# Letting the state space and convolution steps precede the projections in the planner's order

## The chip, the cores and the metric

The kernel runs on one core of a Trainium2 chip. The metric is device microseconds of one execution. Three runs of the kernel before took 1490.85, 1486.84 and 1486.92 us, a median of 1486.92. Engines are called as in the profile: PE is TensorE's matmul side (PEld its weight loads), DVE is VectorE, ACT is ScalarE, POOL is GpSimd and SP is the engine whose queue issues nearly all DMAs.

## The reference, cut to what matters

Two layers run over 256 latent and 256 context tokens of width 1024. The change lies in the mixer of layer 0:

```python
p_lat = h_lat @ w_in                      # 1024 -> 3*768 + 256; the same for the context tokens
u = p[..., -256:]                         # to the state space branch (S5)
st_f, st_b = s5_scan(u, ...)              # 16 groups, 64 complex states, both directions
y_s5 = s5_readout(u, st_f, st_b, ...)     # gelu, then a gated linear unit
uc = short_conv(p[..., :3 * 768], ...)    # three taps, then x1, x2, v of 768 channels each
z = x1 * fft_conv(v, kf[:, 0], bias[0])   # a long convolution by transform, product, inverse
y_hy = x2 * fft_conv(z, kf[:, 1], bias[1])
x = x + m[2] * (concat([y_hy, y_s5]) @ w_out)
```

A mixture of experts, layer 1 (a gated recurrence and its own experts) and a norm follow; the change does not touch their code.

## The kernel before, in words

Everything is kept transposed, channels on the 128 partitions and the 512 tokens along the free dimension. Weights of the projections are split into two parts (`whi` on ACT, `wlo` on POOL or DVE), and each product is three matmuls of 128x512.

`layer0_mixer` (L1304) runs two streams of work. The **fill** (`pipeline`, L1265) is a list of independent jobs: `Channels` (L1162) computes 128 channels of the in projection with the short convolution, `Mods` (L1203) multiplies a block of the modulation weights, `Out` (L1225) computes 128 columns of the out projection from some of the 8 channel blocks. Each job splits its weights (`prep`), runs its matmuls (`mms`) into one of two PSUM banks `in_t`, and finishes on ACT, DVE and POOL (`after`). The **main** stream is a chain. First comes the state space branch `s5_mixer` (L889), four quarters of four groups each: tables `Gt` on DVE and `Hm` on POOL (`s5_quarter_tables`, L822), the product `U`,`Gm` and the scan on DVE that ends in `prev` (`s5_state`, L971), the matrix `Km` (matmuls `Hm`,`wB`, copied to `KX` and moved by 8 DMAs of SP, L874), and the readout `U`,`Km` and `prev`,`Hm`; then `s5_glu` (L931). Then `convs` (L1438) takes six units of 128 channels in the order 4, 5, 0, 1, 2, 3. A unit is two convolutions (`hyena_conv`, L1090): matmuls `zv`,`dft`, a stretch of DVE work (`Z`, `t`, `Z`, `yy`) with two products `t` on POOL, and the inverse matmuls `yy`,`dft`. In between it computes the filter of the unit after it (`hyena_spectra`, L1036: tiles `hw`, `sd`, `nv`, `K`).

`drive` (L209) writes the two streams into one program: it takes a step of the main stream, which ends in a `yield` of some microseconds, then takes jobs of the fill until their own estimates make up that gap. The gaps are 5.0 (L911), 4.5 (L913), 3.8 (L927) and less in a quarter, 6.5 (L1118) after the products of a convolution, 0.9 and 0.8 in between. The gaps of the state space part add up to 63.4, the fill jobs listed first (10 `Channels` of 5.12 and 8 `Mods` of 1.83) to 65.8. The gaps of the convolutions add up to 100.2, the fill left for them (without the last eight `Out` jobs, which need unit 3) to about 101.

The order on each engine is not the order of the program alone. A planner gives each instruction a number as it is written and plays the program through a model of the machine; whenever an engine is free there, it takes the ready instruction with the lowest number. The order that results is fixed: on the chip each engine works through its queue, and an instruction whose input is late holds those behind it. `E.first()` (L126) rewinds the counter to zero for the instructions written inside it, and restores it after. The kernel before uses it in the start of layer 0, in the routing and in layer 1, not in `drive`.

Of the kernel before, what the change touches and what calls it, by code (L numbers as in the profile page):

```python
# [2 lines left out]

# [1 line left out]

# [183 lines left out]
def run(g):  # L189
    for _ in g:  # L190
        pass


def steps(g, n):
    for _ in range(n):
        next(g, None)
# [9 lines left out]
        yield  # L206


def drive(main, fill):  # L209


    for gap in main:
        while gap > 0:
            c = next(fill, None)
            if c is None:
                break
            gap -= c
# [12 lines left out]
def mm3(E, o, w, h, ks, n0=0, n=T, first=True, last=True):  # L230

    for i, k in enumerate(ks):
        E.mm(o, w[0][:, k, :], h[0][:, k, n0:n0 + n], first and i == 0, False)
        E.mm(o, w[0][:, k, :], h[1][:, k, n0:n0 + n], False, False)
        E.mm(o, w[1][:, k, :], h[0][:, k, n0:n0 + n], False, last and i == len(ks) - 1)
# [653 lines left out]
def s5_mixer(E, o, hT, ycat, tabs, ws, hp, tp, wp):  # L889

    inp = []
    for m in range(2):
        b = E.bank("s5")
        mm3(E, b, ws[m], hT, range(KD))
        uT = wp.tile([P, T], F32, tag="uT", name="uT")
        E.act(uT, b, AF.Copy)
        yield 0.7
        if m == 0:
            Gm = next(tabs)
        inp.append((yield from s5_input(E, o, m, uT, wp, tp)))  # L900
    for m in range(2):
        U, ud = inp[m]
        y = wp.tile([P, 8, 64], F32, tag="uT", name="y5")
        for i in range(2):
            q = 2 * m + i
            if q:
                Gm = next(tabs)
                yield 1.2
            sl = slice(4 * i, 4 * i + 4)
            prev = s5_state(E, o, q, U[:, sl], Gm, wp)  # L910
            yield 5.0  # L911
            Hm, Km = next(tabs)
            yield 4.5  # L913
            b = E.bank("s5")
            for g in range(4):
                oo = b[:, g * 64:(g + 1) * 64]
                E.mm(oo, Km[:, g, :], U[:, 4 * i + g, :], True, False)
                E.mm(oo, Hm[:, 0, g, :], prev[:, 0, g, :], False, False)
                E.mm(oo, Hm[:, 1, g, :], prev[:, 1, g, :], False, True)
            E.tt(y[:, sl], b[:, :256].rearrange("p (g c) -> p g c", c=64), ud[:, sl], ADD)  # L920
            if i == 1:
                yield 0.7
                yield from s5_output(E, m, y, ycat, tp)
            if q < 3:
                tabs = s5_quarter_tables(E, o, q + 1, hp, tp)
                next(tabs)
                yield 3.8  # L927
    E.dump('ys5', ycat[:, 6:8])


def s5_glu(E, ycat, tp):  # L931
    gw = tp.tile([P, 2, 512], F32, tag="Gt", name="gw")
    E.SY.dma_start(gw, E.a['s5_glu_w'][0].rearrange("(k p) n -> p k n", p=P))
    yield 0
    glb = E.prm['glb']
    ag = []
    for m in (2, 3, 0, 1):
        b = E.bank("s5")
        for k in range(2):
            E.mm(b, gw[:, k, m * P:m * P + P], ycat[:, 6 + k, :], k == 0, k == 1)  # L940
        ag.append(b)
    for m in range(2):
        sg = tp.tile([P, 512], F32, tag=f"t{'xy'[m]}", name="sg")
        E.act(sg, ag[m], AF.Sigmoid, bias=glb[:, 2 + m:3 + m])
        E.stt(ycat[:, 6 + m, :], ag[2 + m], glb[:, m:m + 1], sg, ADD, MUL)


def s5_input(E, o, m, uT, wp, tp):

    UT = tp.tile([64, 8, 8, 16], F32, tag="Gt", name="UT")  # L950
    uv = uT.rearrange("p (c j) -> p j c", j=8)
    for h in range(2):
        b = E.bank("s5")
        for i in range(4):
            E.tr(b[:64, i * P:(i + 1) * P], uv[:, 4 * h + i, :])
        E.copy(UT[:, :, 4 * h:4 * h + 4, :].rearrange("p g j n -> p j g n"),
               b[:64].rearrange("p (j g n) -> p j g n", j=4, g=8))
    yield 1.5
    U = wp.tile([P, 8, 64], F32, name="U", bufs=2)
    b = E.bank("s5")  # L960
    for g in range(8):
        E.tr(b[:, g * 64:(g + 1) * 64], UT[:, g].rearrange("p j n -> p (j n)"))
    bv = b.rearrange("p (g c) -> p g c", c=64)
    E.act(U[:, :, 0:32], bv[:, :, 32:64], AF.Copy)
    E.act(U[:, :, 32:64], bv[:, :, 0:32], AF.Copy)
    ud = wp.tile([P, 8, 64], F32, name="ud", bufs=2)
    E.tt(ud, U, bcast(o.dcol[:, 8 * m:8 * m + 8], 2, 64), MUL, E.G)
    return U, ud
# [47 lines left out]
def s5_output(E, m, y, ycat, tp):  # L1016
    E.act(y, y, AF.Gelu_apprx_tanh)
    yield 0.8
    YT = tp.tile([64, 8, 8, 16], F32, tag="Gt", name="YT")
    for h in range(2):  # L1020
        b = E.bank("s5")
        for i in range(4):
            E.tr(b[:64, i * P:(i + 1) * P], y[:, 4 * h + i, :])
        E.copy(YT[:, :, 4 * h:4 * h + 4, :].rearrange("p j g n -> p g j n"),
               b[:64].rearrange("p (g j n) -> p g j n", g=4, j=8))
    yield 1.5
    b = E.bank("s5")
    for j in range(8):
        E.tr(b[:, j * 64:(j + 1) * 64], YT[:, j].rearrange("p g n -> p (g n)"))
    bv = b.rearrange("p (j s c) -> p s c j", j=8, s=2)  # L1030
    yv = ycat[:, 6 + m, :].rearrange("p (s c j) -> p s c j", s=2, j=8)
    E.act(yv[:, 1], bv[:, 0], AF.Copy)
    E.act(yv[:, 0], bv[:, 1], AF.Copy)
# [270 lines left out]
def layer0_mixer(E):  # L1304
    class O:
        pass
    o = O()
# [6 lines left out]
    with ExitStack() as l0:  # L1314
        E.psum(l0, "left", **{"in": (1, 2), "tr": (1, 1)})
        pl = l0.enter_context(E.pool("p_l0", 1))
        ycat = pl.tile([P, KD, T], F32, name="ycat")
# [4 lines left out]
        hT = [p_h.tile([P, KD, T], F32R, tag=f"h{i}", name=f"h0_{i}") for i in range(2)]  # L1322
# [3 lines left out]
        hp = E.hp = s5s.enter_context(E.pool("s5h", 1, "right"))  # L1326
        tq = E.tq = s5s.enter_context(E.pool("s5t", 1, "right"))
# [59 lines left out]
        with E.pool("boot", 1) as E.bp, E.pool("s5a", 1, "right") as E.tp:  # L1387
            tabs, ws = boot(E, o, feed, hT, hdn2)
# [7 lines left out]
        def more():  # L1396
            yield from first
            yield from jobs
            yh.extend(p_h.tile([P, KD, T], F32R, tag=f"h{i}", name=f"yh{i}") for i in range(2))
            for ks in ((4, 5, 6, 7), (0, 1), (2,), (3,)):  # L1400
                for i in range(8):
                    yield Out(E, feed, i, ks, yh, ycat, tmp, lambda ks=ks: done.issuperset(ks), tail if ks[0] == 3 else None)
                if ks[0] in (4, 0):
                    yield between.pop(0)
                    yield between.pop(0)
# [15 lines left out]

        fill = pipeline(more())
        wp = s5s.enter_context(E.pool("s5w", 1, "right"))
        drive(s5_mixer(E, o, hT, ycat, tabs, ws, hp, tq, wp), fill)
        drive(s5_glu(E, ycat, tq), fill)
        done.update((6, 7))
        s5s.close()
        hys = ExitStack()
        E.psum(hys, "right", hs=(2, 1), pd=(1, 3))
        with hys, E.pool("hyzb", 2, "right") as zb, E.pool("hyk", 2, "right") as kp, E.pool("hyt", 1, "right") as tp, \  # L1430
                E.pool("hyw", 2, "right") as wp:
            zp.update({u: zb for u in (0, 1)})
            E.dft = zb.tile([P, 8, P], F32, name="dft", bufs=1)
            E.SY.dma_start(E.dft, a['k_dft'])
            order = (4, 5, 0, 1, 2, 3)
            filt = {}

            def convs():  # L1438
                for _ in hyena_spectra(E, 4, hdn2, kp, tp, filt):
                    yield 3.0  # L1440
                for i, u in enumerate(order):
                    if i == 5:
                        tags = {"wge": ("fw3", 512), "bge": ("win", 256), "wA": ("hw", 1024), "lT": ("so", 512)}
                        ends["r"] = Route(E, 0, T // P, E.mT[0], lambda nm: tp.tile([P, tags[nm][1]], F32, tag=tags[nm][0], name=nm))
                        ends["r"].prepare(E.bank("hs")[:, 0])
                    spec = hyena_spectra(E, order[i + 1], hdn2, kp, tp, filt) if i < 5 else iter(())
                    steps(spec, 1)
                    while ("x1", u) not in zt:
                        next(fill)
                    yield from hyena_unit(E, u, *filt[u], zt["v", u], zt["x1", u], ycat, wp, spec)  # L1450
                    done.add(u)
                    run(spec)
                    yield 0.5

            drive(convs(), fill)
            run(fill)
    E.dump('ycat', ycat)
    E.dump('x1', E.xT)
# [677 lines left out]
def kernel(ctx: ExitStack, tc: tile.TileContext, a, out, dbg=None, stop=None):  # L2136
# [9 lines left out]
    with E.pool("ring", 3) as E.ring, E.pool("mod", 1) as E.mod:  # L2146
        layer0_mixer(E)
# [45 lines left out]
```

## Time and profile before

| | |
|---|---|
| median of 3 runs | 1486.92 us |
| the profiled execution, device time | 1486.51 us |
| its span | 1484.7 us |
| granted clock of PE, mean over the span | 0.932 |
| PE busy over the span | 87% |
| DVE, POOL, ACT busy over the span | 55%, 27%, 26% |

The span is the profiled part of an execution; 1.8 us of the device time lie around it. Busy shares are averages over stages with different limits. A row of the timeline gives the start in us from the span's start, the length, the engine, the line, the operation, the tile written and those read, the shape, how many were merged, and in brackets how long the engine had been idle before it and for whom. A granted clock of 1.00 is the full 2.4 GHz of PE, 0.50 the half.

### The profile page before, as it was taken

The page shows a single profiled execution, that of the slowest core. Times are in us where ns is not written, and L with a number is a line of the kernel's source. Part 1 is how long each engine was busy: PE and PEld are TensorE (multiplying, and loading weights), DVE is VectorE, ACT ScalarE, POOL GpSimd, SP SyncE. Part 2 cuts the span into 40 slices and gives each one's busy share as a digit, 9 for nine tenths or more (in the row PEclk, how much of TensorE's full clock was granted, in tenths as well). Part 3 has the DMA queues.
Part 4 walks back from the last instruction along what each step waited for, and adds up shares of the span by engine and source line. Part 5 has one row for each costly group of instructions (what it writes and reads, how often), then busy time and mean ns, then how long its engine had stood idle before and what let it go on. Part 6 is the DMA issues. An engine that isn't in the chain of part 4 may idle for free. (4 is left out here: it accounts for less than half of the span.)

```text
span 1484.7 us, 18755 instructions
## 1 busy us (share of the span) xinstructions
PE 1285.4 (87%) x7093; PEld 826.7 (56%) x7093; DVE 809.5 (55%) x1785; ACT 387.5 (26%) x655; POOL 400.0 (27%) x326
## 2 busy tenths in 40 slices
PE   6499999898886769999999498979798969999995
PEld 4266766575665443444444277878778733444443
DVE  5856554766666453344335685665656553343443
ACT  2233433132232321111111443333333312121211
POOL 2733431334554321111100452323231221111101
PEclk9699999899988779999999698999999979999998
DMA  8415673145121389999994111211213189999970
GB/s 298 181 57 183 225 259 142 57 144 218 42 91 79 117 340 416 393 388 384 383 385 175 43 62 53 78 64 59 84 60 122 65 339 395 418 419 420 419 314 31
DMA packets 55747, 311.91 MB, mean 210 GB/s; under 512 B 14441, under 2 KB 19994, under 8 KB 24282
## 3 DMA queue, kind: packets, MB, share of 16 engines
q1 hardware_dynamic: 50746, 303.72, 52.2%
q0 software_dynamic: 4608, 6.30, 1.3%
q8 instruction: 61, 1.00, 0.3%
q10 hardware_dynamic: 288, 0.52, 0.1%
q14 instruction: 44, 0.36, 0.1%
HBM read 315.76 MB, written 4.19 MB: 215 GB/s over the span
## 5 line engine op out<-in xcount | busy, mean ns | idle before, releaser
L148 PE MATMUL pg_t<-w,Xe 128*64 128x512 f32 x1024 | 228.7, 599 | 0.0
L148 PE MATMUL in_t<-h,whl 128*128 128x512 f32 (+1 forms) x768 | 147.2, 349 | 3.2 <-DVE h L158 2.4
L148 PEld LDWEIGHTS pg_t<-w,Xe 128*64 128x64 f32 x1024 | 71.1, 138 | 135.7 <-issue 131.1
L161 POOL TENSOR_TENSOR whl<-wraw,whl 128x2048 fp32r<-128x2048 f32 x20 | 93.6, 4684 | 175.6 <-ACT whl L155 175.6
L148 PEld LDWEIGHTS in_t<-h,whl 128*128 128x128 f32 x768 | 121.7, 195 | 22.1 <-POOL h L161 3.1
L148 PE MATMUL py_t<-w,hid 128*64 128x512 f32 x512 | 119.1, 606 | 4.2 <-DVE yl L161 3.0
L164 DVE SCALAR_TENSOR_TENSOR sg<-sg,ws,pg_t 128x256 f32<-128x256 f32 x32 | 15.4, 480 | 180.2 <-ACT sg L155 180.2
L1615 POOL MEMSET Xg<- 128x1024 f32 x32 | 30.4, 959 | 295.6 <-PE ga_t L152 295.6
L164 DVE SCALAR_TENSOR_TENSOR xT<-sc_t,mT,xT 128x256 f32<-128x256 f32 x204 | 90.3, 479 | 29.6 <-PE sc_t L148 28.1
L161 POOL TENSOR_TENSOR wlo<-w,whi 128x1024 fp32r<-128x1024 f32 (+3 forms) x51 | 72.0, 1416 | 107.6 <-ACT whi L155 100.7
L148 PE MATMUL sc_t<-OT,yh 128*128 128x512 f32 (+1 forms) x256 | 90.7, 369 | 10.2 <-DVE xT L164 7.6
L148 PE MATMUL in_t<-h,whi 128*128 128x512 f32 x288 | 97.6, 416 | 2.1 <-ACT ms L155 1.4
L148 PE MATMUL sc_t<-OT,yl 128*128 128x512 f32 (+1 forms) x256 | 82.6, 337 | 0.0
L148 PEld LDWEIGHTS sc_t<-OT,yh 128*128 128x128 f32 x256 | 48.0, 188 | 54.2 <-issue 27.9
L148 PEld LDWEIGHTS py_t<-w,hid 128*64 128x64 f32 x512 | 34.1, 138 | 64.8 <-issue 55.9
L155 ACT ACTIVATE yh<-py_t 128x1024 fp32r<-128x1024 f32 (+1 forms) x34 | 33.1, 974 | 121.5 <-PE py_t L148 117.3
L168 DVE TENSOR_SCALAR OT<-ht_t,ksq 128x512 fp32r<-128x512 f32 (+1 forms) x32 | 19.7, 616 | 81.5 <-PE ht_t L148 81.5
L155 ACT ACTIVATE sg<-pg_t 128x256 f32<-128x256 f32 x32 | 12.3, 385 | 195.3 <-PE pg_t L148 195.2
L148 PEld LDWEIGHTS in_t<-h,whi 128*128 128x128 f32 x288 | 51.5, 190 | 17.9 <-issue 5.2
L148 PE MATMUL at_t<-QA,X 128*128 128x128 f32 x224 | 37.5, 318 | 26.9 <-DVE QA L161 26.9
L1670 POOL DMA_INDIRECT Xg<-rows,ix x32 | 32.3, 1010 | 104.9 <-DVE ws L1676 33.4
L148 PE MATMUL in_t<-whl,h 128*128 128x256 f32 x384 | 56.5, 300 | 3.7 <-POOL whl L161 3.7
(442 smaller groups left out, 2446.1 us busy)
## 6 DMA issues: line engine op xcount, KB each, us to landing
w<-in_w_gu_dram SPq DMA_DIRECT2D x128, 1024.0 KB
w<-in_w_dn_dram SPq DMA_DIRECT2D x64, 1024.0 KB
w<-in_w_mod_dram SPq DMA_DIRECT2D x24, 2048.0 KB
wraw<-in_w_in_dram SPq DMA_DIRECT2D x20, 1024.0 KB
w<-in_w_in_dram SPq DMA_DIRECT2D x5, 2048.0 KB
w<-in_w_out_dram SPq DMA_DIRECT2D x2, 2048.0 KB
cwo<-in_w_out_dram SPq DMA_DIRECT2D x2, 2048.0 KB
rows<-hh SPq DMA_DIRECT2D x6, 512.0 KB
```

What stands on the lines that cost most here:

```text
L148: self.TE.matmul(o, l, r, start=st, stop=sp)
L155: self.S.activation(o, i, f, **k)
L161: (e or self.V).tensor_tensor(o, x, y, op=op)
L164: self.V.scalar_tensor_tensor(o, x, s, y, op0=op0, op1=op1)
L168: (e or self.V).tensor_scalar(o, x, s1, None, op0=op0)
L1615: E.G.memset(X, 0.0)
L1670: E.G.indirect_dma_start(X, None, rows, bass.IndirectOffsetOnAxis(ix[:, pi:pi + 1], 0), bounds_check=n - 1, oob_is_err=False)
```

## The change

`drive` takes an argument `E`. With it, each step of the main stream is written inside `E.first()`, so that its instructions get numbers from zero on; the fill keeps its numbers. The order in which the program is written, the gaps, the jobs, the tiles and the instructions stay. The three calls in layer 0 (state space, gated unit, convolutions) pass `E`; there is no other caller.

```diff
-def drive(main, fill):
-
-
-    for gap in main:
+def drive(main, fill, E=None):
+
+
+    while True:
+        with E.first() if E else nullcontext():
+            gap = next(main, None)
+        if gap is None:
+            return
         while gap > 0:
             c = next(fill, None)
             if c is None:
...
-        drive(s5_mixer(E, o, hT, ycat, tabs, ws, hp, tq, wp), fill)
-        drive(s5_glu(E, ycat, tq), fill)
+        drive(s5_mixer(E, o, hT, ycat, tabs, ws, hp, tq, wp), fill, E)
+        drive(s5_glu(E, ycat, tq), fill, E)
...
-            drive(convs(), fill)
+            drive(convs(), fill, E)
             run(fill)
```

## Rows read from the trace of the kernel before

**Rows 1.** The page's head and part 1: busy us, share of span, instructions.
```profile
span 1484.7 us, 18755 instructions
...
PE 1285.4 (87%) x7093; PEld 826.7 (56%) x7093; DVE 809.5 (55%) x1785; ACT 387.5 (26%) x655; POOL 400.0 (27%) x326
```
**Rows 2.** Windows: stretch, length, busy us per engine, granted clock, DMA share, GB/s.
```profile
80.00:240.00 160.00, 153.81 (x1007) 110.83 (x1006) 82.98 (x144) 56.03 (x96) 58.93 (x38) 1.00 0.51 186
240.00:475.00 235.00, 206.92 (x972) 146.16 (x972) 155.67 (x329) 62.23 (x119) 97.33 (x77) 0.92 0.30 110
475.00:512.00 37.00, 26.12 (x137) 13.87 (x137) 15.53 (x36) 9.23 (x21) 16.36 (x18) 0.82 0.13 38
```
**Rows 3.** Waits of PE, 240 to 475: us in total, times, longest.
```profile
PE pd_t L148 <- DVE yy L161: 15.0, 6, 4.0
PE hs_t L148 <- DVE hw L161: 11.3, 5, 3.3
```
**Rows 4.** Timeline of PE: one quarter of the state space branch.
```profile
169.25 1.90 PE L148 MATMUL s_t<-U,Gm 128*128 128x64 f32 x16
...
177.09 0.55 PE L148 MATMUL s_t<-Hm,wB 64*16 64x112 f32 x4
...
191.90 0.33 PE L148 MATMUL s_t<-U,Km 128*128 128x64 f32 x2
```
**Rows 5.** Timeline of SP's queue: the DMAs of that quarter.
```profile
180.81 7.64 SPq L874 DMA_DIRECT2D Km<-KX  x8
```
**Rows 6.** Timeline of PE: one inverse of a convolution.
```profile
364.70 1.13 PE L148 MATMUL pd_t<-yy,dft 128*128 128x256 f32 x4 [2.64 <-DVE yy L161]
365.48 1.10 PE L148 MATMUL in_t<-yh,whi 128*128 128x512 f32 x2
...
372.05 1.02 PE L148 MATMUL pd_t<-yy,dft 128*128 128x256 f32 x4
```
**Rows 7.** Timeline of PE: first, eleventh and twelfth wait, and what follows.
```profile
266.73 1.99 PE L148 MATMUL hs_t<-fw,hdn 64*128 64x256 f32 x4 [3.13 <-DVE hw L161]
...
465.11 2.93 PE L148 MATMUL pd_t<-yy,dft 128*128 128x256 f32 x6 [4.00 <-DVE yy L161]
...
473.39 1.46 PE L148 MATMUL pd_t<-zv,dft 128*128 128x256 f32 x6
481.31 3.78 PE L148 MATMUL pd_t<-yy,dft 128*128 128x256 f32 x8 [6.47 <-DVE yy L161]
485.78 0.74 PE L152 MATMUL tr_t<-ksq,yo 128*128 128x128 f32 x4 [0.69 <-ACT yo L155]
488.16 0.76 PE L148 MATMUL in_t<-yh,whi 128*128 128x512 f32 x2 [1.63 <-ACT yh L155]
489.51 0.79 PE L148 MATMUL in_t<-yh,whi 128*128 128x512 f32 x1 [0.59 <-POOL yh L161]
...
496.04 0.73 PE L148 MATMUL in_t<-yh,whi 128*128 128x512 f32 x2
```
**Rows 8.** Timeline of PE: the start of the state space branch.
```profile
83.99 0.50 PE L148 MATMUL in_t<-h,wlo 128*128 128x512 f32 x1 [1.32 <-POOL wlo L161]
...
88.97 0.73 PE L148 MATMUL s_t<-h,whi 128*128 128x512 f32 x2
```
**Rows 9.** Timeline of POOL: splits of weights and the start of a table.
```profile
66.02 2.38 POOL L161 TENSOR_TENSOR wlo<-w,whi 128x1024 fp32r<-128x1024 f32 x1
...
154.59 1.29 POOL L161 TENSOR_TENSOR Hm<-ux,uy 128x512 f32<-128x512 f32 x1 [0.52 <-PE s_t L148]
...
176.82 2.60 POOL L161 TENSOR_TENSOR wlo<-w,whi 128x1024 fp32r<-128x1024 f32 x1
```
**Rows 10.** Timeline of DVE: the end of the scan in two quarters.
```profile
177.25 3.90 DVE L161 TENSOR_TENSOR prev<-tA,tB 64x256 f32<-64x256 f32 x6
...
210.66 1.85 DVE L161 TENSOR_TENSOR prev<-tA,tB 64x256 f32<-64x256 f32 x6
```
**Rows 11.** Timeline of PE: the norm of the first filter.
```profile
252.43 1.95 PE L148 MATMUL hs_t<-ones,hw 128*128 128x1 f32 x16 [0.85 <-ACT hw L155]
```

More of the change, by code (lines that the diff above doesn't have):

```diff
@@ L1 @@
 import math
-from contextlib import ExitStack
+from contextlib import ExitStack, nullcontext
 import numpy as np
```

## The prediction, made before the changed kernel ran

> **What bounds the kernel now.** I read the page first: PE is busy 87% of the span [rows 1], so a reordering inside one stage can give back only what PE loses there. Then the windows of the stage that the change touches [rows 2]. From 80 to 240 us, beside the state space branch, PE is busy 153.8 of 160 us at the full clock: this stretch is bound by PE's work, and moving its steps changes the order of the work, not its amount. From 240 to 475 us, beside the convolutions, PE is busy 206.9 of 235 and its granted clock is 0.92: 28.1 us idle, and 16% of the time at the lower of the two levels. From 475 to 512 us it is busy 26.1 of 37 at 0.82. DMA is far from full in all three. So what can be won is at most the 6.2, 28.1 and 10.9 us idle and half of what runs at the lower clock.
>
> The waits say for whom PE idles [rows 3]: 15.0 us for `yy` in 6 waits and 11.3 us for `hw` in 5. The timeline shows that there is one such wait per convolution, twelve in all; the first eleven add up to 26.3 us, 2.4 each, the twelfth is 6.47 [rows 7]. Behind the waiting matmuls the fill follows, as at 365.48 [rows 6], with its inputs long ready: the planner put the main step at the head of PE's queue when its model had the input ready, and on the chip the input came later.
>
> **What the change moves.** No instruction is added or removed. It decides only where a main step and a fill step are both ready and the fill was written first. Where is that so in the trace?
>
> *State space.* In the third quarter the matmuls of `Km` start at 177.09, 5.9 us after `U`,`Gm` ended at 171.15 [rows 4], though they need only `Hm` and a free buffer; the gap of 5.0 stands between them in the program. In the four quarters the distance is 5.5, 7.3, 5.9 and 3.2 us (the row of one stands for the pattern). `Km` then takes 8 DMAs, 7.64 us of issue [rows 5], and its readout starts at 191.90. With the change these matmuls go right behind `U`,`Gm`, so each quarter shortens by about 4 to 8 us; with the second input block, whose matmuls at 88.97 can go some 5 us earlier [rows 8], I estimate the branch to end about 30 us sooner, near 210 instead of 240.
>
> *Convolutions.* At 364.70 four of the eight inverse matmuls run, then the fill until 372.05, then the other four [rows 6]: 6.3 us lost to the chain, the gap of 6.5. Four of the twelve inverses are split in this way by 6 to 7 us, and two start 4 to 5 us after `yy` (the row of one stands for the pattern). That is about 35 us of chain. Together the last convolution would end some 60 us earlier, near 425 instead of 485.
>
> That is time of the chain, not of PE, which runs the fill meanwhile. It is worth what PE loses at the end, where the fill is used up. After 473.39 nothing of the fill is left; PE waits 6.47 us for `yy`, 0.69, 1.63 and 0.59 us for the steps behind it, and runs at half clock until 496.04 [rows 7]. With 60 us of fill behind the chain this is what goes:
> - the twelfth wait becomes one like the others: 6.47 - 2.39 = 4.1 us;
> - 0.69 + 1.63 + 0.59 = 2.9 us;
> - 489.51 to 496.04 at full instead of half clock: 6.5 / 2 = 3.2 us.
>
> At the start, PE waits 1.32 us for the first `wlo` of the fill while the matmuls of 88.97 stand by [rows 8]; their weights were split by 68.4 [rows 9]. They can fill it: 1.3 us. The gains add up to 11.5 us.
>
> The eleven waits stay. They are the chip's lateness against the planner's model along the chain, and the chain has as many steps as before.
>
> **What it costs.** A main step that had the fill as cover now waits on PE at the instant at which the model has it ready, and all that is queued on PE waits with it.
>
> *Scan.* `Km` was last in the quarters; with it earlier, `prev` is. Its six operations take 1.85 us in one quarter and 3.90 in another [rows 10], where POOL was splitting weights at the same time [rows 9]. If the model has the short value, PE waits up to 2.1 us a quarter for this, and up to 4 if another DVE step is hit as well; it may also wait for nothing, as it does not wait at any readout now. I take 1.0 us, four times: 4 us, with bounds of 0 and 16.
>
> *Small steps of a unit.* `zv` to the second convolution, `yo` to its transposes, `hw` to the norm: three in each of six units, 18 in all, which mostly have cover now. The one that waits, waits 0.85 us [rows 11]; the others nothing. Bounds 0 and 15 us; I take 0.13 each, 2.4 us, near the many that do not wait.
>
> *Other queues.* On SP the DMAs of `Km` and the loads of the filters pass loads of fill weights, by up to 7.64 us [rows 5]; no wait of PE for a weight load shows in the three stretches, since three buffers run ahead, so nothing; without that cover it would be 7.6 us a quarter. On POOL the table operations from 154.59 on [rows 9] (five more behind it, 7 us) pass splits of the fill; they did so already, and PE's waits for `wlo` are 2.0 us in 80 to 240. Nothing, with 6 us as the upper bound. On DVE and ACT the main steps were mostly written ahead of the fill beside them. Nothing below zero is excluded: after the change more of the convolutions run beside `Channels`, and the first four waits, which lie there, average 2.0 us against 2.6 for the next seven. That could give 4 us; I leave it in the range.
>
> The sum: -11.5 + 4 + 2.4 = -5.1 us on the profiled execution, 1486.51 - 5.1 = 1481.4 us. That execution lies 0.4 us under the median of the runs, which I neglect: **1481 us**. What comes after the mixer starts earlier by the same amount and is otherwise the same.
>
> A rule of the Trainium skill speaks against this change: TensorE: Matmul & The Clock Gate (The mechanism) states that matmuls are in strict order in start and end, with no reordering. By it every main matmul placed too early holds all of the fill behind it, as the rows show at 465.11 [rows 7], and moving 30 more steps to their earliest place would only add waits: that is the third rival below.
>
> **The rivals.**
>
> *It gains more.* The waits shrink, since the chain now runs beside `Channels` with fewer operations on POOL per matmul, and fewer of them drop the clock. Against it: the first four convolutions already run there and wait 2.0 us on the mean, 3.13 in the first [rows 7]. If twelve waits of 1.2 us remain, 14 us go of the idle time and some 5 us of half clock besides, less than the full cost of the new waits: 1466 us.
>
> *It does almost nothing.* The planner already takes the main step first at most places, since the main stream runs behind the program; what moves is chain time which PE does not feel, and the end is bound by the last `Out` jobs, each with a split and an addition on POOL, instead of by the chain. For it speaks that eleven of twelve waits are already at the instant of readiness. 1486 us, give or take 4.
>
> *It is slower.* The mechanism is the one of the cost part: on PE's queue in order, steps that had the gaps as cover now each hold the fill. Four quarters with three steps each (`Gt`, `U`,`Gm`, readout) and 18 small ones make 30 places. At 0.85 us each [rows 11], 25 us, and the clock, which is at 1.00 from 80 to 240 now [rows 2], may fall after the longer ones. Against 11.5 us of gain it decides from 0.38 us per place on. At 0.7 us it gives 21 - 11.5 = +9.5: 1496 us. Against it: at the readouts, which interrupt a fill job in all four quarters and so were placed at the instant of readiness, PE does not wait now.
>
> **How the numbers follow.** A measurement of this kernel can tell about 0.3%, 4.5 us, from no change: faster is under 1482.5, slower over 1491.4. The forecast (1474 to 1487 by the nearer bounds of its costs) has a chance of 0.42, the larger gain 0.14, nothing 0.21, slower 0.23. The forecast falls on the faster side with 0.31 of its 0.42 and within with the rest, nothing falls within, with 0.02 on either side, and slower is over the bound with 0.21: faster 0.47, same 0.30, slower 0.23. The range goes from 1465, just under the larger gain, to 1497, just over the slower case.
>
> **What would show it.** In the profile after: the matmuls `Hm`,`wB` within 2 us of `U`,`Gm`; the last `s_t` readout before 200 us; no inverse split by fill; the last `pd_t<-yy` before 440 us, and a stretch of `Out` jobs behind it in which PE is busy throughout at clock 1.00; the last transpose of the mixer (510.4 us before) near 505. About twelve waits of PE on `yy` and `hw`, 25 to 30 us in all. It is wrong if PE's idle time from 80 to 240 grows beyond 12 us, if the chain's end does not move by 30 us or more, or if the chain ends early and PE still idles in the last 40 us.

## The result, and the profile after

| | before | after |
|---|---|---|
| median of 4 runs | 1487.47 us (1486.84 to 1490.85) | 1531.46 us (1529.14 to 1532.78) |
| ratio after to before | | 1.0289, 95% interval 1.0268 to 1.0311 |
| span of the profiled execution | 1484.7 us | 1527.4 us |

The change makes the kernel 44 us slower. The forecast was 1481, with a range up to 1497; sign and size were both wrong.

Of the page of the changed kernel, the line that answers to [rows 1]:

```profile
span 1527.4 us, 18764 instructions
...
PE 1313.1 (86%) x7093; PEld 833.9 (55%) x7093; DVE 814.8 (53%) x1785; ACT 387.1 (25%) x655; POOL 398.9 (26%) x326
```

The same 7093 matmuls now keep PE busy 27.7 us longer. That is the first hint: there are no more of them, so some took longer. The windows of the changed kernel, PE alone (stretch, length, busy us and matmuls, granted clock, DMA share, GB/s), to be held against [rows 2]:

```profile
50.00:80.00 30.00, 10.72 (x45) 0.56 0.19 70
80.00:240.00 160.00, 147.33 (x812) 0.85 0.30 107
240.00:475.00 235.00, 208.47 (x993) 0.96 0.38 141
475.00:512.00 37.00, 31.92 (x142) 0.81 0.15 57
```

and the first of these stretches in the kernel before:

```profile
50.00:80.00 30.00, 15.88 (x57) 0.63 0.19 71
```

Busy time times clock says how much work PE got done. From 80 to 240 us it was 153.81 x 1.00 = 153.8 before and is 147.33 x 0.85 = 125.2 now; from 50 to 80 it was 10.0 and is 6.0. At 240 us the changed kernel is therefore 32.6 us of PE work behind. The matmul counts agree, roughly, since some records are missing: 812 against 1007. Beside the convolutions the clock is better than before, 0.96 against 0.92. The last transpose of the mixer starts at 552.22 instead of 510.40, 41.8 us later: that is nearly all of the loss, and what follows only shifts. The product is a rough measure. Matmuls that take longer because they are dealt out among others, as those of the quarters below, count as more work in it; summed from 50 us to the end of the mixer it gives 386 us now and 375 before, for the same matmuls. The true lag at 240 us is therefore rather more than 32.6.

**The start of the branch.** Timeline of PE in the changed kernel, the first quarter's transposes of `Gt` between the matmuls of the first input block:

```profile
74.11 0.45 PE L152 MATMUL s_t<-ksq,Gt 128*128 128x128 f32 x1 [12.83 <-DVE Gt L161]
74.21 0.78 PE L148 MATMUL s_t<-h,whi 128*128 128x512 f32 x1
74.78 0.41 PE L152 MATMUL s_t<-ksq,Gt 128*128 128x128 f32 x1
...
81.21 0.44 PE L152 MATMUL s_t<-ksq,Gt 128*128 128x128 f32 x1 [3.88 <-DVE pt L158]
```

and the same place in the kernel before:

```profile
71.50 0.80 PE L148 MATMUL s_t<-h,wlo 128*128 128x512 f32 x1 [9.26 <-DVE wlo L161]
```

Before, the 24 matmuls of the input block ran first and the transposes came behind them. Now the second step's transposes have the same low numbers as the first step's matmuls and are shuffled among them, so the matmuls wait with them, at 74.11 and again at 81.21: 12.83 and 3.88 us, where PE idled 9.26 us before.

**The quarters.** The run of main matmuls behind `UT` in the first quarter, with the two windows around it. Before, `U`,`Gm` took 1.90 us in one piece (third quarter) and the fill followed [rows 4]:

```profile
103.72 0.43 PE L148 MATMUL s_t<-U,Gm 128*128 128x64 f32 x2
104.08 0.55 PE L148 MATMUL s_t<-Hm,wB 64*16 64x112 f32 x4
...
106.59 0.43 PE L148 MATMUL s_t<-U,Gm 128*128 128x64 f32 x2
106.96 0.21 PE L148 MATMUL s_t<-C,wB 128*16 128x16 f32 x2
...
112.51 1.05 PE L148 MATMUL in_t<-h,whi 128*128 128x512 f32 x2
...
117.27 0.62 PE L148 MATMUL in_t<-h,whi 128*128 128x512 f32 x2
```

```profile
100.00:110.00 10.00, 10.00 (x81) 1.00 0.57 210
110.00:120.00 10.00, 10.00 (x37) 0.66 0.15 28
```

From 103.72 to 111.49 PE runs nothing but narrow matmuls (64, 112 and 16 columns) of two steps, dealt out alternately. It is never idle, and still the granted clock falls: the first pairs of wide matmuls behind take 1.05 us, those from 117.27 on 0.62. The other three quarters mix the two steps in the same way, from 129, 168 and 196 us; in the second and the fourth PE also waits for `Hm` inside the run, up to 2.92 and 1.34 us.

### The profile page after: what moved, and what is told of

Same layout as the page of the kernel before. It is cut to its first block, busy times and chain, and to the rows that moved or that the text cites. A ratio compares the mean times of both kernels' runs of the same rounds, so it can differ in the third digit from the quotient of the medians.

```text
span 1527.4 us, 18764 instructions
## 1 busy us (share of the span) xinstructions
PE 1313.1 (86%) x7093; PEld 833.9 (55%) x7093; DVE 814.8 (53%) x1785; ACT 387.1 (25%) x655; POOL 398.9 (26%) x326
## 5 line engine op out<-in xcount | busy, mean ns | idle before, releaser
L148 PE MATMUL in_t<-h,whi 128*128 128x512 f32 x288 | 103.1, 431 | 7.3 <-ACT ms L155 5.7
L164 DVE SCALAR_TENSOR_TENSOR xT<-sc_t,mT,xT 128x256 f32<-128x256 f32 x204 | 90.3, 479 | 29.6 <-PE sc_t L148 28.1
L148 PE MATMUL in_t<-w,sc 128*32 128x512 f32 x384 | 66.0, 685 | 5.2 <-DMA w<-in_w_mod_dram 5.2
L148 PE MATMUL in_t<-h,wlo 128*128 128x512 f32 x144 | 60.8, 422 | 0.8 <-POOL wlo L161 0.8
```

What stands on the lines that cost most here:

```text
L148: self.TE.matmul(o, l, r, start=st, stop=sp)
L164: self.V.scalar_tensor_tensor(o, x, s, y, op0=op0, op1=op1)
```

## The experiments

Numbers behind a run are its median and the difference to the runs of the kernel before on the same chip (medians of 1487.2 to 1487.8 us).

### The two stages apart

Theory K said that the loss is made in the state space stage, Theory Y that it is made beside the convolutions. The first run gives precedence to the branch alone:

```diff
-            drive(convs(), fill, E)
+            drive(convs(), fill)
```

> Precedence in the state space branch and its gate alone; the convolutions keep their numbers. Theory K (the loss is made between 60 and 240 us, where the narrow matmuls of U,Gm and Hm,wB stand together with no wide fill between them and the granted clock is at its lower level in four stretches): by the sum of busy time times clock over the windows, the changed kernel is 32 us of PE work behind at 240 us. So 1515 to 1525, with the clock from 80 to 240 near 0.85 as in the changed kernel. Theory Y (the loss is made beside the convolutions, where the yo transposes wait for the bank tr that the fill holds): under 1500.

Measured: 1515.32, +28.1 (ratio 1.0186, 1.0169 to 1.0203), clock 0.85 from 80 to 240. The second gives it to the convolutions alone (`E` taken from the calls with `s5_mixer` and `s5_glu`):

> Precedence beside the convolutions alone. Theory K: the state space stage is as before (PE busy near 154 us from 80 to 240, clock 1.00) and the whole lies within 10 us of the kernel before, 1480 to 1497. Theory Y: 1505 to 1525, with the yo transposes 10 us or more behind the inverse they belong to, as in the changed kernel.

Measured: 1493.90, +6.7 (1.0025 to 1.0059). So 28 of the 44 us belong to the branch, and Theory K names the larger part. The convolutions lose too, where a gain had been forecast, and 9 us appear only when both are done.

### What costs in the state space stage

First the numbering: main steps count on from step to step, so that no step passes an earlier one of the chain.

```diff
         with E.first() if E else nullcontext():
+            if E:
+                E.tc.cur_priority = getattr(E, 'count', 0)
             gap = next(main, None)
+            if E:
+                E.count = E.tc.cur_priority
```

> Precedence everywhere, but the numbers of the main steps go on from step to step instead of starting again at zero, so that the steps keep their own order. Theory M (a later step's first instructions pass an earlier step's last ones, and this mixing of the chain with itself is what costs): near 1500 or under, with no wait of 12.8 us for Gt at 74 us. Theory K: U,Gm and Hm,wB still stand together, as one run of 5 to 6 us of narrow matmuls instead of 8 to 14; the clock falls behind them still, so 1510 to 1525, the wait at the start (some 7 us) being all that goes.

Measured: 1522.74, +35.5. The wait of 12.8 us at 74 is gone and PE's work from 50 to 90 us is back (23.87 x 0.73 = 17.4; before 24.26 x 0.72 = 17.5; changed 18.53 x 0.59 = 10.9). Mixing was a part, not the whole. Now the step of `Km` alone, the one behind the gap of 5.0, gets its own number back:

```diff
-        with E.first() if E else nullcontext():
-            gap = next(main, None)
+        with E.first() if E and last != 5.0 else nullcontext():
+            gap = last = next(main, None)
```

> As the changed kernel, but the step that makes Km (24 narrow matmuls, 4 readouts of banks, 8 DMAs) keeps its own number, so that the fill stands between U,Gm and Hm,wB as it did before. Theory K: the clock from 80 to 240 is back above 0.95 and 20 to 25 us come back: 1506 to 1512. Theory M or Y: 1520 to 1531, since the start and the convolutions are as in the changed kernel.

Measured: 1513.93, +26.7, a little over the range: 17.5 us of the 44 come back by leaving one step out of four per quarter where it was. The windows from 80 to 240 of the two runs, own order and then `Km` at its own number:

```profile
80.00:240.00 160.00, 148.17 (x906) 0.92 0.41 148
```

```profile
80.00:240.00 160.00, 143.86 (x917) 0.94 0.43 160
```

Both hold the clock better than 0.85, neither as well as before, and the second leaves PE idle for 16 us. Is it the order on PE that lets the clock fall? The next run has no precedence at all and only moves the fill's place in the program:

```diff
-                yield 1.2
+                yield 0
...
-            yield 5.0
+            yield 0
             Hm, Km = next(tabs)
-            yield 4.5
+            yield 10.7
```

> The kernel before, without any precedence; only the fill's place in the program is moved: the gaps of 1.2 and 5.0 ahead of and behind U,Gm become 0 and the 4.5 behind Hm,wB becomes 10.7, so that the transposes of Gt, U,Gm and Hm,wB stand together on PE in each quarter as they do in the run with the steps in their own order. Theory K (narrow matmuls in one run, with no wide fill between, let the clock fall, whatever put them there): the clock from 80 to 240 falls to 0.90 to 0.95 and the time is 1495 to 1510. Rival (the precedence on DVE, ACT, POOL and SP costs the time, and the order on PE is innocent): 1484 to 1491, clock 1.00.

Measured: 1487.19, no difference (0.9991 to 1.0010). Theory K in this plain form falls. Its second quarter, and its window from 80 to 240:

```profile
126.24 1.04 PE L152 MATMUL s_t<-ksq,Gt 128*128 128x128 f32 x8
127.21 1.04 PE L148 MATMUL in_t<-w,sc 128*32 128x512 f32 x2
128.18 2.00 PE L148 MATMUL s_t<-U,Gm 128*128 128x64 f32 x16
130.11 0.55 PE L148 MATMUL s_t<-Hm,wB 64*16 64x112 f32 x4
...
133.35 1.07 PE L148 MATMUL in_t<-w,sc 128*32 128x512 f32 x8
```

```profile
80.00:240.00 160.00, 152.21 (x985) 0.99 0.47 173
```

`U`,`Gm` and `Hm`,`wB` stand together for 5.2 us with no fill between, and the clock holds. The same matmuls in the run with precedence and own order:

```profile
118.53 0.63 PE L152 MATMUL s_t<-ksq,Gt 128*128 128x128 f32 x4 [0.85 <-DVE Gt L161]
119.00 1.00 PE L148 MATMUL s_t<-U,Gm 128*128 128x64 f32 x8
119.93 0.36 PE L148 MATMUL s_t<-Hm,wB 64*16 64x112 f32 x2
121.07 0.36 PE L148 MATMUL s_t<-Hm,wB 64*16 64x112 f32 x2 [0.78 <-POOL Hm L161]
121.36 1.10 PE L148 MATMUL s_t<-U,Gm 128*128 128x64 f32 x8
...
126.46 1.22 PE L148 MATMUL in_t<-h,whi 128*128 128x512 f32 x2
```

The order differs little: the wide matmuls at 127.21 are not there, and the first four of `Hm`,`wB` stand amid `U`,`Gm`. What else differs is that each step stands at the instant at which the planner had its input ready, so PE waits 0.85 us for `Gt` ahead of the run and 0.78 for `Hm` inside it. From `U`,`Gm` on the run takes 7.5 us instead of 5.2, in part because the clock falls within it, and two wide matmuls behind it take 1.22 us. In the changed kernel the mixing did most of the stretching: the same 64 matmuls took 7.8 us without a wait. If that is so (Theory W), wide work between the steps must hold the clock. Each `Km` step of the run with own order gets 8 wide matmuls ahead of it:

```diff
         b, b2 = E.bank("s5"), E.bank("s5")
+        for k in range(KD if g2 == 0 else 0):
+            E.mm(b, E.hT[0][:, k, :P], E.hT[0][:, k, :], True, True)
```

> As the run in which the steps keep their own order with precedence everywhere, but each quarter's Km step begins with 8 wide matmuls of 512 columns (32 in all, their result is not used). They add 32 x 0.23 = 7.4 us of PE work at the full clock. Theory W (the clock falls where narrow matmuls and short waits of PE for Gt and Hm stand together; wide work between them holds it up): the clock from 80 to 240 goes from 0.92 to 0.97 or more, at 240 us as many useful matmuls are done as without them or more, and the time is 1512 to 1524 in spite of the added work. Rival (the waits themselves, or the other queues, make the loss, and the clock only follows): clock as before, time 1527 to 1532.

Measured: 1514.17, 8.6 us less than without the 32 added matmuls, and the clock from 80 to 240 is 0.97 instead of 0.92:

```profile
80.00:240.00 160.00, 149.95 (x933) 0.97 0.38 136
```

Wide work between the steps brings the clock back, as Theory W said. But PE's waits for `Hm`, 2.0 us in this window without the added matmuls, are gone as well, so the run does not tell the narrow matmuls from the waits between them. By these windows the added 7.4 us about eat up what the clock gives back until 240 (145.5 - 7.4 = 138.1 us of useful work, against 136.3), so most of the 8.6 us came later; by what is not shown.

Next, precedence in the branch alone, own order, and `Km` at its own number (the two edits above together):

> Precedence in the state space branch alone, its steps in their own order (numbers go on), and the Km step at its own number: no mixing, no wait for Gt at 74 us, fill between U,Gm and Hm,wB. If mixing, the start and the narrow runs are all of the 28 us that the branch cost alone, 1486 to 1493. If the steps' precedence on DVE also costs (the fill's evictions wait behind the scan's operations and PE waits for the bank, 4.8 us twice in the earlier run with Km at its own number), 1495 to 1505.

Measured: 1502.67, +15.1. Mixing, the start and the narrow runs make up 28.1 - 15.1 = 13.0 us; the rest is another thing. Its timelines of DVE and of PE in the first quarter:

```profile
106.81 0.73 DVE L164 SCALAR_TENSOR_TENSOR ycat<-in_t,pt,ycat 128x510 f32<-128x510 f32 x1
107.47 3.35 DVE L161 TENSOR_TENSOR prev<-tA,tB 64x256 f32<-64x256 f32 x6
110.84 2.19 DVE L164 SCALAR_TENSOR_TENSOR ycat<-in_t,pt,ycat 128x510 f32<-128x510 f32 x3
```

```profile
106.65 0.36 PE L148 MATMUL s_t<-Hm,wB 64*16 64x112 f32 x2
111.74 1.19 PE L148 MATMUL in_t<-h,whi 128*128 128x512 f32 x2 [4.72 <-DVE ycat L164]
```

The fill's job is emptied from its bank by one operation of ACT and two of DVE; those two write `ycat`. With precedence the six operations of `prev` stand between them; the bank stays full, and the next fill matmul waits 4.72 us and starts at the lower clock. No main matmul gains by it: the readout that needs `prev` starts at 127.84. The Trainium skill (PSUM — Partial Sum Buffer, Engine vs sequencer instructions) says that VectorE's queue is strictly first in, first out; the rows at 107.47 and 110.84 agree. To test it, in this stage the fill's evictions get precedence as well:

```diff
     def after(self):
...
-        E.act(y, self.b, AF.Identity, scale=..., bias=...)
-        E.stt(yv[:, :, 1:], ...)
-        E.stt(yv[:, :, :255], ...)
+        with E.first() if E.early else nullcontext():
+            E.act(y, self.b, AF.Identity, scale=..., bias=...)
+            E.stt(yv[:, :, 1:], ...)
+            E.stt(yv[:, :, :255], ...)
```

> As the run with precedence in the state space branch alone, its steps in their own order and Km at its own number (1502.7), but in that stage the operations that empty the fill's banks (one of ACT and two of DVE for each job, and the sums of a modulation job) have precedence too. Theory D (of the branch's loss that is left, most is the fill's evictions queued on DVE behind the scan and prev, for which PE waits 4.7 and 4.3 us, with the clock falling behind): these two waits go, PE's busy time from 80 to 240 is back above 151 us, and the time is 1486 to 1494. Rival (the shift of the loss is elsewhere: DMAs of Km, POOL, or less fill left in front): 1498 to 1504.

Measured: 1490.54, +2.9 (1.0008 to 1.0034). The window, and the two waits of PE that the theory named (us in total, times, longest), first in the run before this one, then here:

```profile
80.00:240.00 160.00, 151.50 (x996) 1.00 0.49 184
```

```profile
PE in_t L148 <- DVE ycat L164: 5.7, 3, 4.7
PE tr_t L152 <- DVE m L428: 4.3, 1, 4.3
```

```profile
PE tr_t L152 <- DVE m L428: 2.2, 1, 2.2
...
PE in_t L148 <- DVE ycat L164: 1.3, 3, 0.7
```

Theory D holds: 12.1 us were the evictions queued behind the scan. Of these, 6.5 us are the two waits; by busy time times clock the window gains 10.7 us (145.11 x 0.97 = 140.8 in the run before). So the branch's 28 us are about 13 for the steps' order on PE and 12 for DVE, in the order in which they were undone; 3 remain.

### Beside the convolutions

With precedence there alone, the last inverse came 17 us before that of [rows 7], and the end of the mixer 6 us later than before. Timeline of PE in that run:

```profile
464.42 3.78 PE L148 MATMUL pd_t<-yy,dft 128*128 128x256 f32 x8 [3.68 <-DVE yy L161]
...
483.36 3.64 PE L148 MATMUL in_t<-w,sc 128*32 128x512 f32 x16 [5.50 <-DMA w<-in_w_mod_dram]
...
490.17 0.63 PE L152 MATMUL tr_t<-ksq,yo 128*128 128x128 f32 x4
...
516.47 0.27 PE L152 MATMUL pd_t<-ksq,ssq 128*128 128x128 f32 x1
```

and the load of those weights on SP's queue:

```profile
475.52 0.33 SPq L174 DMA_DIRECT2D w<-in_w_mod_dram  x1
```

The last `yo` is transposed 25.8 us behind its inverse; before it was 4.5 us. The bank `tr` is one buffer that `hyena_unit`, `Channels` and `Mods` share in the order of the program, whatever their numbers. A main step that is early still waits for every fill step written ahead of it that uses the bank, here for two modulation jobs, and the second of these waits 5.50 us for weights, whose load was issued at 475.52, as soon as the first job's matmuls were done. The edit: `yo` goes to a bank `pd`, which only the main stream and the final norm use.

```diff
     yield 0.8
-    b = E.bank("tr")
+    b = E.bank("pd")
```

> Precedence beside the convolutions alone, and the yo transposes of each unit go into a bank pd, which the fill does not use, instead of tr. Theory Y: with precedence alone the last inverse started at 464.4 us, 17 us before that of the kernel before, but its yo transposes only at 490.2, behind the transposes of two modulation jobs in the one bank tr, the second of which waited 5.5 us for its weights. Without that wait the last yo transposes start near 469, the mixer ends 5 to 15 us before its 516.5, and the time is 1479 to 1489, against 1493.9. Rival (the end is set by the late weights and by the Out jobs, not by the bank): 1490 to 1495.

Measured: 1488.32, 5.6 us less than without this edit and level with before (0.9995 to 1.0014). The control, the kernel before with the same bank:

> The kernel before, with the yo transposes in a bank pd, as the control for the two runs with that bank. Its yo transposes start 2 to 6 us behind their inverses already, so the bank is hardly ever held: 1483 to 1490 by every theory. A gain above 5 us here would mean that the bank helps by itself.

Measured: 1489.38, no difference (0.9996 to 1.0017). In the run with precedence and the bank, the last inverse starts at 439.69, 41.6 us before that of the kernel before; what holds the end now are the weights of the last modulation jobs:

```profile
439.69 2.94 PE L148 MATMUL pd_t<-yy,dft 128*128 128x256 f32 x8 [3.50 <-DVE yy L161]
...
454.96 3.23 PE L148 MATMUL in_t<-w,sc 128*32 128x512 f32 x16 [6.34 <-DMA w<-in_w_mod_dram]
...
479.79 3.64 PE L148 MATMUL in_t<-w,sc 128*32 128x512 f32 x16 [6.48 <-DMA w<-in_w_mod_dram]
```

Two of the three weight buffers hold the out projection by then; the second job of a pair can load only when the first is done. So the pairs are spread over the Out jobs:

```diff
                     yield Out(...)
-                if ks[0] in (4, 0):
-                    yield between.pop(0)
-                    yield between.pop(0)
+                    if ks[0] in (4, 0) and i % 4 == 3:
+                        yield between.pop(0)
```

> Precedence beside the convolutions, yo in a bank pd, and the last four modulation jobs one after every fourth Out job instead of in pairs. In the run without this last edit the last inverse started at 439.7 us, 42 us before that of the kernel before, and PE waited 12.8 us in two waits for the weights of the second job of each pair. Theory Y2 (the gain forecast for the end is there once neither the bank nor the late weights hold it): the two waits go, the mixer ends near 499 instead of 511, 1472 to 1479. Rival (the Out jobs and their splits on POOL set the end anyway): 1485 to 1489.

Measured: **1473.57**, -14.0 (0.9891 to 0.9920): faster than both kernels. Its mixer ends at 498.70, and the two waits for weights are down to 2.6 and 1.8 us:

```profile
440.33 3.78 PE L148 MATMUL pd_t<-yy,dft 128*128 128x256 f32 x8 [3.61 <-DVE yy L161]
...
459.73 1.92 PE L148 MATMUL in_t<-w,sc 128*32 128x512 f32 x16 [2.62 <-DMA w<-in_w_mod_dram]
...
498.70 0.27 PE L152 MATMUL pd_t<-ksq,ssq 128*128 128x128 f32 x1
```

The control has both mends and no precedence:

> The control: the kernel before with yo in a bank pd and the modulation jobs spread in the same way, no precedence. By Theory Y2 its last inverse stays near 481 and sets the end, 1484 to 1490. If the spreading helps by itself, 1475 to 1483.

Measured: 1493.71, +6.1 (1.0027 to 1.0051), a little above the range expected; its last inverse starts at 487.64, later than before. So the mends alone bring nothing and even cost 6 us, for a reason that stays open. Against this control, precedence beside the convolutions is worth 20 us with both mends, nothing that can be told with the bank alone (1488.32 against 1489.38), and costs 7 without either.

### Both stages together

The changed kernel with `yo` in a bank `pd`:

> The changed kernel, with the yo transposes in a bank pd. Theory Y: the convolutions no longer wait for the fill at yo, above all the 34 us from the inverse at 305 to the transposes at 339, and the two stages' losses no longer reinforce each other: 1505 to 1518 against 1531. Rival (units 0 and 1 wait for their inputs from the fill, which is 32 us behind, so that the bank changes little): 1524 to 1531.

Measured: 1550.00, +62.2, which neither theory had. Its chain is done earlier, the last `yo` transposed at 483.61 instead of 525.76, and its mixer ends later, at 572.35: fill was left over, and the end is fill. An early chain is worth nothing while the fill is far behind. The windows say where the fill fell back further than in the changed kernel: from 240 to 475 us PE is busy 201.3 us at a clock of 0.92, against 208.5 at 0.96, some 15 us of work less; and PE waits 12.8 us for the weights of modulation jobs instead of 5.2. What slowed PE from 240 to 475 is not settled, nor where the 9 us come from that only the two halves together cost. With every mend, in both stages:

> Precedence in both stages, with every mend that the runs before pointed to: own order and Km's own number and the evictions first in the state space stage, beside the convolutions yo in a bank pd and the modulation jobs spread. If Theory D holds and the two stages add up, 1473.6 plus what the run with the evictions first loses against the kernel before: 1472 to 1481. If the branch's precedence brings something of its own by an earlier start of the convolutions, under 1470. Rival (the stages reinforce each other's loss, as the 44 us of the change against 28 and 7 of its halves suggest): above 1485.

Measured: 1478.36, -9.3 (0.9906 to 0.9954). 1473.6 + 2.9 = 1476.5 was due, so the halves about add up here, and precedence in the branch has nothing of its own to give.

## Why the prediction was wrong

**"Changes the order of the work, not its amount."** This step failed. It took the 153.8 us of PE work from 80 to 240 at clock 1.00 [rows 2] for a property of the stage. It was one of the order: in the kernel before, each step came when its input was there, with wide fill around it. Moved ahead of the fill, the steps brought waits, the mixing and the lower clock: 28.6 us of PE work are lost from 80 to 240 and 4.0 ahead of it, the mixing not counted. (Fill between `U`,`Gm` and `Hm`,`wB` was not needed for the full clock: the run that only moved the gaps lost nothing.) The price of a step was sought in waits alone. PE's idle time in that stretch did rise over the 12 us named as the sign of error, to 12.7, but that is 6.5 more; the clock took 0.15 x 147 = 22.

**"Each quarter shortens by about 4 to 8 us."** `Hm`,`wB` did start within 2 us of `U`,`Gm`, as the first sign asked, in fact in the middle of it. But the last readout is at 218.27, not before 200 (221.18 before). The text took numbers from zero to mean "ahead of the fill"; they also mean "level with every other main step".

**The price of the scan (4 us, at most 16) and of the small steps (2.4, at most 15).** Mis-sized, and the sentence behind them, that DVE and ACT had the main steps written first anyway, was wrong: `prev` passing the fill's second eviction cost 4.72 us at one place, and the evictions 12 us in all, the clock included. The scan was asked how long PE waits for it, not who waits behind it on DVE.

**SP and the weights at nothing.** Wrong in its size: PE waited 5.2 us for modulation weights at 520.20 in the changed kernel, and 12.8 us in the run with precedence beside the convolutions and the bank alone. The changed kernel's last inverse and this wait:

```profile
501.45 3.78 PE L148 MATMUL pd_t<-yy,dft 128*128 128x256 f32 x8 [3.67 <-DVE yy L161]
...
520.20 3.29 PE L148 MATMUL in_t<-w,sc 128*32 128x512 f32 x16 [5.24 <-DMA w<-in_w_mod_dram]
```

Three buffers ran ahead only as long as the out projection did not hold two of them.

**The gain of 11.5 us at the end.** The changed kernel has none of it: its last inverse starts at 501.45, 20 us later than before, not 60 us earlier. The mechanism was right, and a step was missing: the bank `tr` was not in the text. With the bank and the weights out of the way the last inverse starts at 440.33 (forecast: near 425) and waits 3.61 us instead of 6.47, no wait for `yo` or `yh` follows it, the mixer ends 11.7 us earlier, and the kernel gains 14.0 us. Of the signs, in the changed kernel no inverse is split by more than 2.3 us from its first matmul to the start of its last piece; before, five were split by 6.0 to 7.7 us, where the prediction counted four. Its waits for `yy` and `hw` from 240 to 475 us fell to 6.1 and 4.6 us, against 15.0 and 11.3 in [rows 3], so the eleven waits were not a fixed price. But others came, 6.4 us for `dg` and 3.6 for `ms`, and PE idles 26.5 us in that stretch instead of 28.1.

**The rivals.** The one that came true is "it is slower". It named the queue of PE in strict order and a clock that may fall, and put 0.7 us on each of 30 places, 1496. It had the sign and not the size: what a wait lets happen to the clock, and a queue other than PE's, were not in its price. The rule beside it, matmuls in strict order (the Trainium skill, TensorE: Matmul & The Clock Gate, The mechanism), agrees with the rows: at 111.74, in the run with precedence in the branch alone, own order and `Km` at its own number, all of PE stood behind one matmul for 4.72 us. This rival carried 0.23.

## What to carry to other kernels

Before a stream is given precedence, list for each of its steps every queue and every buffer that it shares with the stream that it passes: precedence moves instructions, but a shared buffer still goes round in program order, and an eviction that is passed on DVE stops the matmuls of the other stream. Leave filler around small steps, so that their inputs are there when PE comes to them: steps placed too early brought waits here, and the clock fell. Give precedence only where PE idles; and when numbers are rewound, let them count on, so that a chain doesn't overtake itself.

## What was not expected of the hardware

The granted clock fell while PE was busy without a gap, behind 7.8 us of matmuls of 16 to 112 columns (0.66 from 110 to 120 us in the changed kernel); behind 5.2 us of the same matmuls, with wide ones ahead of them, it held, and where PE waited 0.85 us ahead of them and 0.78 us among them it fell again. The runs do not tell what of this, the narrow matmuls or the waits, made it fall in the last case. A busy share of 10.00 of 10 us is no sign of the full clock.
